# Weights of the next projection loaded from mid-block, and two token tiles multiplied per weight page, in a diffusion block on one core

## The chip, the core and the metric

The kernel runs on one core of one Trainium2 chip. TensorE (PE in the profile) multiplies into PSUM, of which the kernel keeps eight tiles of 128 x 512 float32 here (called banks below); VectorE (DVE), ScalarE (ACT) and GpSimd (POOL) do the rest; the sync engine (SP) issues nearly all transfers, from one queue. The order of the instructions on each engine is fixed when the program is built, so an instruction that waits holds up what stands behind it on its engine. The metric is the device time of one execution in microseconds (us); lower is better.

## What is computed

One layer of a diffusion backbone over 1024 latent tokens and 256 context tokens, width 1024. What matters here is its first third:

```python
mod = jax.nn.silu(c) @ w_mod[layer] + b_mod[layer]        # 6 rows of 1024; and the same for c_ctx
h = modulate(rmsnorm(x, norm1_g[layer]), sh1, sc1)        # 1024 tokens
hc = modulate(rmsnorm(ctx, norm1_g[layer]), sh1c, sc1c)   # 256 tokens
(q_na, k_na, v_na, q_g, k_g, v_g, og, z_lr, m_a, m_b) = jnp.split(h @ w_in[layer], IN_OFFSETS, axis=-1)
q_na = rmsnorm(heads(q_na, NA_HEADS), na_q_norm_g[layer])   # k_na likewise, also for the context
z = jnp.einsum('bldr,drk->bldk', z_lr, w_alpha) + b_alpha   # GLA gates, two directions
la = jnp.maximum(jax.nn.log_sigmoid(z) / GLA_GATE_TAU, GLA_LOG_ALPHA_MIN)   # then cumulated along each chunk
```

Behind it come neighbourhood attention, gated linear attention, the merge, and a SwiGLU network, none of which the change touches.

## The kernel before

Every float32 product is made of three products of a high and a low part (`mm3`): hi·hi, hi·lo and lo·hi. One 128 x 1024 slice of weights comes as a "page": a transfer into a tile `raw` (three buffers), a cast to `w_hi` on ScalarE and a subtraction to `w_lo` on VectorE, both written into tiles with the tag `w`.

The token-major projections are five jobs, `q`, `k`, `v`, `gqk` and `gv`, each 512 columns of `w_in` in four pages (two of the eight steps `k` of the inner dimension per page). Job `q` goes over 8 token tiles of 128, the others over 10 (the last two are context). For one token tile, TensorE runs 24 matmuls of 512 columns (8 steps times 3) into one PSUM bank, tile `psj`; the result then goes through ScalarE and VectorE, for `q` and `k` a norm per head (`norm_heads`: square `sq`, sum, a power on GpSimd, product `st`, copy), and is stored to DRAM. At the start of a job its four pages are loaded and split. The pool `wp` has eight `w` tiles, of which three pages take six (a high and a low part each), and the fourth page takes the two of the pool `jp`. So the next job's page 0 can be split while a job runs, and its other pages only as the running job's last token tile is done with pages 0, 1 and 3.

Two strands of side work are woven in, one step of each per token tile from job `k` on. `mod_units` sums four rows of the modulation vector, each over eight pages `wm` of `w_mod` on VectorE (`acc`), and after the eighth splits the sum into `parts`, adds over partitions with four matmuls (tile `mp`, one PSUM bank) and copies the row out (`mr`). `gate_units` first loads the low-rank gate input (`za`) and the gate weights (`w2r`) and splits them, then makes for each of four `a` three matmuls (tile `psl`, the same bank as `mp`), a clamp on VectorE (`la`), exponential and logarithm on ScalarE, cumulated sums (`cum`) on VectorE, and exponentials again. A scheduler sets the final order of each engine from the order in which the program is written and from its own estimates.

Of the kernel before, what the change touches and what calls it, by code (L numbers as in the profile page):

```python
# [10 lines left out]
F32 = mybir.dt.float32  # L11
# [7 lines left out]
P = 128  # L19
# [3 lines left out]
KT = D // P  # L23
NT = T // P
# [21 lines left out]
NWX = 1  # L46
# [28 lines left out]
CX = 1  # L75
ZH = 4
MID = 6
FK = 1
FQ = 1
FE_ = 1  # L80
# [12 lines left out]
def hybrid_block_kernel(  # L93
# [115 lines left out]
            src, hi = src[part], hi[part]  # L209
        (lo_eng or DVE).tensor_tensor(lo, src, hi.bitcast(F32), op=ALU.subtract)  # L210

    def load_page(pl, src, k0, per, ncols, tag, scale_row=None, lo_eng=None, after=None, bufs=8):
        raw = rawp.tile([P, per, ncols], F32, tag="raw", name="raw")
        SP.dma_start(raw, src[k0 * P:(k0 + per) * P, :].rearrange("(k p) n -> p k n", p=P))
        if scale_row is not None:
            POOL.tensor_tensor(raw, raw, scale_row.unsqueeze(1).broadcast_to([P, per, ncols]), op=ALU.mult)  # L216
        hi = pl.tile([P, per, ncols], F32R, tag=tag, name="w_hi", bufs=bufs)
        lo = pl.tile([P, per, ncols], F32R, tag=tag, name="w_lo", bufs=bufs)
        hi_lo(hi, lo, raw, lo_eng, after)
        return hi, lo  # L220
# [6 lines left out]
    def cut(w, s):  # L227
        return (lambda k: w[0](k)[:, s]), (lambda k: w[1](k)[:, s])

    def mm3(ps, ks, st, mv, first=True, last=True):  # L230
        sh, sl = st
        vh, vl = mv
        ks = list(ks)
        for k in ks:
            PE.matmul(ps, sh(k), vh(k), start=first and k == ks[0], stop=False)
            PE.matmul(ps, sh(k), vl(k), start=False, stop=False)
            PE.matmul(ps, sl(k), vh(k), start=False, stop=last and k == ks[-1])
# [14 lines left out]
    with ExitStack() as sa:  # L252
# [11 lines left out]
        jps = sa.enter_context(pool("jps", NJ, space=PSUM))  # L264

        def h_tok(t):
            if t < NT:
                s = slice(t * P, (t + 1) * P)
                return (lambda k: hh[:, k, s]), (lambda k: hl[:, k, s])
            s = slice((t - NT) * P, (t - NT + 1) * P)  # L270
            return (lambda k: hch[:, k, s]), (lambda k: hcl[:, k, s])
# [102 lines left out]
        mps = sa.enter_context(pool("mps", space=PSUM))  # L374
        jpb = sa.enter_context(pool("jpb", 7 - NJ, space=PSUM))
# [27 lines left out]
        def mod_units():  # L403
            for s in range(4):
                acc = jp.tile([P, D], F32, tag="acc", name="acc", bufs=1)
                POOL.memset(acc, 0.0)
                SP.dma_start(acc[0:1], b_row[0:1, (2 + s) * D:(3 + s) * D])
                for k in range(KT):
                    wm = jp.tile([P, D], F32, tag="wm", name="wm2", bufs=3)
                    SP.dma_start(wm, w_mod[k * P:(k + 1) * P, (2 + s) * D:(3 + s) * D])  # L410
                    DVE.scalar_tensor_tensor(acc, wm, cs[:, k, 0:1], acc, op0=ALU.mult, op1=ALU.add)
                    if k == KT - 1:
                        for c in range(2):
                            c_ = slice(c * 512, (c + 1) * 512)
                            parts = [page("parts", F32R, tag=tg) for tg in ("st", "sb")]
                            hi_lo(parts[0], parts[1], acc[:, c_])
                            mp = mps.tile([P, 512], F32, tag="mp", name="mp2")
                            for u in range(2):
                                PE.matmul(mp, ones_r, parts[u], start=u == 0, stop=u == 1)
                            mr = page("mr2", tag="sb")  # L420
                            ACT.copy(mr[0:1], mp[0:1])
                            SP.dma_start(mod_d[s:s + 1, c_], mr[0:1])
                    yield


        def gate_stream():
            wz_raw = jp.tile([P, KT, 32], F32, name="wz_raw", bufs=1)
            SP.dma_start(wz_raw, w_in[:, 3072:3104].rearrange("(k p) n -> p k n", p=P))
            wz = jp.tile([P, KT, 64], F32R, name="wz", bufs=1)
            hi_lo(wz[:, :, 0:32], wz[:, :, 32:64], wz_raw)  # L430
            for a, b, n, i0, o in ((hh, hl, 512, 0, 0), (hh, hl, 512, 512, 512), (hch, hcl, 256, 0, 1024)):
                ps = jps.tile([P, 512], F32, tag="j", name="psz")
                for k in range(KT):
                    PE.matmul(ps[0:64, 0:n], wz[:, k, :], a[:, k, i0:i0 + n], start=k == 0, stop=False)
                    PE.matmul(ps[0:64, 0:n], wz[:, k, :], b[:, k, i0:i0 + n], start=False, stop=k == KT - 1)
                sz = jp.tile([P, 512], F32, tag="sq", name="sz")
                ACT.copy(sz[0:64, 0:n], ps[0:64, 0:n])
                DVE.tensor_tensor(sz[0:32, 0:n], sz[0:32, 0:n], sz[32:64, 0:n], op=ALU.add)
                SP.dma_start(z_d[:, o:o + n], sz[0:32, 0:n])
# [29 lines left out]

        def gate_units():  # L470
            gate_parts()
            yield
            for a in range(4):
                back = a % 2
                w2a = w2[:, 2 * a:2 * a + 2].rearrange("p h k -> p (h k)")
                la = jp.tile([P, T + TC], F32, tag="la", name="la", bufs=1)
                for o, n in ((0, 512), (512, 512), (1024, 256)):
                    ps = mps.tile([P, 512], F32, tag="mp", name="psl")
                    PE.matmul(ps[:, 0:n], w2a, zs[:, o:o + n], start=True, stop=True)
                    DVE.tensor_scalar(la[:, o:o + n], ps[:, 0:n], ba[:, a:a + 1], -40.0, op0=ALU.add, op1=ALU.max)  # L480
                    yield
                ACT.activation(la, la, AF.Exp, scale=-1.0)
                ACT.activation(la, la, AF.Ln, bias=1.0)
                yield
                DVE.tensor_scalar(la, la, 1.0 / 16.0, 1.0, op0=ALU.mult, op1=ALU.min)
                cum = jp.tile([P, T + TC], F32, tag="cum", name="cum", bufs=1)
                st_ = slice(None, None, -1) if back else slice(None)
                for o, n, r in ((0, 512, rst), (512, 512, rst), (T, TC, ones[:, 0:1].broadcast_to([P, TC]))):
                    DVE.tensor_tensor_scan(cum[:, o:o + n][:, st_], r, la[:, o:o + n][:, st_], 0.0,
                                           op0=ALU.mult, op1=ALU.add)  # L490
                yield
                nl = small.tile([P, 1], F32, tag="nl", name="nl")
                end = T if back else T + TC - 1
                DVE.tensor_scalar_mul(nl, cum[:, end:end + 1], -1.0)
                ein = jp.tile([P, T + TC], F32, tag="la", name="ein", bufs=1)
                ACT.activation(ein[:, 0:T], cum[:, 0:T], AF.Exp)
                ACT.activation(ein[:, T:], cum[:, T:], AF.Exp, bias=nl)
                SP.dma_start(ein_d[a * P:(a + 1) * P, :], ein)
                ex = cum[:, 0:T]
                ACT.activation(ex, ex, AF.Exp, scale=-1.0)  # L500
                SP.dma_start(ex_d[a * P:(a + 1) * P, :], ex)
                yield

        gus = gate_units()
        mus = mod_units()
        nj = 0
        for job, c0 in (("q", 0), ("k", 512), ("v", 1024), ("gqk", 1536), ("gv", 2048)):
            if job == "q":
                w = qw
            else:  # L510
                pages = [load_page(jp if i >= 4 - NWX else wp, w_in[:, c0:c0 + 512], 2 * i, 2, 512, "w",
                                   bufs=2 * NWX if i >= 4 - NWX else 8)
                         for i in range(4)]
                w = [(lambda k, u=u, pages=pages: pages[k // 2][u][:, k % 2, :]) for u in range(2)]
            if job == "k":
                gate_stream()
            for t in range(NT if job == "q" else NT + NTC):
                if job != "q":
                    next(mus, None)
                    next(gus, None)  # L520
                half = job == "gqk" and t >= NT
                n0 = 256 if half else 0
                if job == "q" and t < NPRE:
                    ps = pre[t]
                else:
                    nj += 1
                    ps = (jps, jpb)[nj % 2].tile([P, 512], F32, tag="j", name="psj")
                    mm3(ps[:, n0:], range(KT), h_tok(t), cut(w, slice(n0, 512)))
                if job == "q":
                    norm_heads(ps, q_d, t)  # L530
                elif job == "k":
# [983 lines left out]
```

## Time and profile before

| | |
|---|---|
| runs shown (3) | median 1658.98 us, 1656.54 to 1659.48 |
| the profiled execution | 1664.38 us, of which the span is 1662.6 |
| mean granted clock of TensorE over the span | 0.975 |
| busy share of the span: PE, DVE, ACT, POOL | 94%, 61%, 38%, 32% |
| the chain that ended last: PE, DVE, DMA, ACT, issue, POOL | 68%, 12%, 8%, 4%, 4%, 3% |
| bytes moved, mean rate | 231.30 MB, 139 GB/s |

The profiled execution is 5.40 us over the median of the runs shown. A granted clock of 1.00 is TensorE's upper level, 2.4 GHz, and 0.50 the lower, 1.2 GHz. The matmul ends in the trace are modelled, so a busy TensorE need not be one at its full rate: start times are what to count from.

### The profile page before, as it was taken

The numbers are of one execution on the slowest core, as the hardware profiler recorded it, in microseconds if no ns is written. First come the engines' busy times: TensorE is split into PE (matmuls) and PEld (weight loads), VectorE is DVE, ScalarE is ACT, GpSimd is POOL, SyncE is SP. The second block draws the span as 40 slices with busy tenths as digits, with TensorE's granted clock in tenths as the row PEclk, the third lists the DMA queues.
The fourth block names the chain that finished last, engine by engine and source line by source line (L and its number), as shares of the span: only waits on it lengthen the run. The fifth ranks groups of instructions, "written<-read, shape, count | busy, mean of one in ns | idle before, by whom it ended". The sixth has DMA issues, their size and how long they took to land.

```text
span 1662.6 us, 21554 instructions
## 1 busy us (share of the span) xinstructions
PE 1566.1 (94%) x7884; PEld 1267.2 (76%) x7884; DVE 1017.9 (61%) x1584; ACT 635.4 (38%) x1219; POOL 532.2 (32%) x354
## 2 busy tenths in 40 slices
PE   6999598999999999999989997999999999999998
PEld 4777376887878787778877875788888888887886
DVE  5755546407877774564457568766666666678356
ACT  4333342217877773222211323333333333344442
POOL 2422000003111211210022335455555555256444
PEclk9999699999999999999999997999999999999999
DMA  9445675425333316335553221232323333684342
GB/s 322 134 146 180 218 226 184 145 81 158 108 108 105 115 52 212 116 136 172 204 184 113 77 88 47 89 107 96 102 95 104 111 113 122 219 287 146 102 146 95
DMA packets 166291, 231.30 MB, mean 139 GB/s; under 512 B 15324, under 2 KB 101276, under 8 KB 166184
## 3 DMA queue, kind: packets, MB, share of 16 engines
q1 hardware_dynamic: 166184, 229.91, 42.9%
q8 instruction: 62, 1.02, 0.3%
q14 instruction: 45, 0.37, 0.1%
HBM read 164.68 MB, written 65.19 MB: 138 GB/s over the span
## 4 chain that ended last, share of the span: by engine, by line
PE 68%; DVE 12%; DMA 8%; ACT 4%; issue 4%; POOL 3%; SPq 1%; DVEq 0%; ACTq 0%; POOLq 0%
PE psdn L136 9%; PE psj L136 9%; PE psd L136 9%; PE fZ L136 7%; PE fX L136 7%; PE fW L136 7%; PE pso L136 5%; PE psb L136 3%; PE fY L136 3%; PE pv L136 2%; DMA raw<-in_w_in_dram 2%; PE pt L136 1%; DMA wm<-in_w_mod_dram 1%; PE mp L136 1%; DVE w_lo L210 1%
## 5 line engine op out<-in xcount | busy, mean ns | idle before, releaser
L136 PE MATMUL psdn<-wd,a 128*128 128x512 f32 x924 | 211.8, 390 | 3.4 <-DVE a L210 1.5
L136 PEld LDWEIGHTS psdn<-wd,a 128*128 128x128 f32 x924 | 172.8, 188 | 42.2 <-DVE a L210 3.4
L210 POOL TENSOR_TENSOR w_P<-sc,w_P 128x512 fp32r<-128x512 f32 x88 | 126.5, 1439 | 107.8 <-ACT w_P L205 100.7
L136 PE MATMUL psj<-w_hi,hh 128*128 128x512 f32 x320 | 129.9, 409 | 12.8 <-ACT w_hi L205 12.4
L210 POOL TENSOR_TENSOR w_lo<-raw,w_hi 128x1024 fp32r<-128x1024 f32 x24 | 57.5, 2398 | 249.2 <-ACT w_hi L205 192.8
L136 PE MATMUL fZ<-T,w_P 128*128 128x512 f32 x528 | 130.6, 397 | 5.6 <-DVE u L1267 5.6
L136 PE MATMUL psd<-hh,w_hi 128*128 128x512 f32 x320 | 134.7, 421 | 0.0
L136 PE MATMUL fX<-B,w_P 128*128 128x512 f32 x528 | 131.7, 398 | 0.7 <-ACT u L1086 0.7
L136 PE MATMUL psj<-w_lo,hh 128*128 128x512 f32 x320 | 129.7, 406 | 2.0 <-DVE w_lo L210 2.0
L210 POOL TENSOR_TENSOR w_P<-raw,w_P 128x512 fp32r<-128x512 f32 x66 | 101.9, 1546 | 90.5 <-ACT w_P L205 90.5
L136 PE MATMUL psd<-hh,w_lo 128*128 128x512 f32 x320 | 128.9, 403 | 0.0
L136 PE MATMUL psd<-hl,w_hi 128*128 128x512 f32 x320 | 128.4, 401 | 0.0
L136 PE MATMUL psj<-w_hi,hl 128*128 128x512 f32 x320 | 127.8, 404 | 0.0
L136 PEld LDWEIGHTS fZ<-T,w_P 128*128 128x128 f32 x528 | 101.1, 192 | 28.6 <-DVE u L1267 6.9
L136 PEld LDWEIGHTS fX<-B,w_P 128*128 128x128 f32 x528 | 100.0, 190 | 24.4 <-ACT u L1086 1.1
L205 ACT CAST w_P<-sc 128x512 fp32r<-128x512 f32 x88 | 54.3, 620 | 138.8 <-PE fZ L136 79.7
L205 ACT CAST w_hi<-raw 128x1024 fp32r<-128x1024 f32 x64 | 66.6, 1048 | 91.0 <-POOL raw L216 40.6
L243 POOL TENSOR_TENSOR r<-r,nhalf 128x8 f32<-128x8 f32 (+1 forms) x40 | 50.5, 1266 | 147.9 <-DVE r L242 147.9
L210 DVE TENSOR_TENSOR a<-ar,a 128x512 fp32r<-128x512 f32 x77 | 60.8, 798 | 59.9 <-ACT a L205 59.6
L205 ACT CAST a<-ar 128x512 fp32r<-128x512 f32 x77 | 47.8, 621 | 112.9 <-PE psdn L136 63.6
L136 PEld LDWEIGHTS psj<-w_hi,hh 128*128 128x128 f32 x320 | 62.2, 195 | 29.3 <-ACT w_hi L205 13.8
L210 DVE TENSOR_TENSOR w_lo<-raw,w_hi 128x1024 fp32r<-128x1024 f32 x40 | 53.0, 1331 | 44.0 <-ACT w_hi L205 43.7
(266 smaller groups left out, 3456.1 us busy)
## 6 DMA issues: line engine op xcount, KB each, us to landing
wm<-in_w_mod_dram SPq DMA_DIRECT2D x48, 512.0 KB
raw<-in_w_in_dram SPq DMA_DIRECT2D x40, 512.0 KB
ar<-s_d SPq DMA_DIRECT2D x77, 256.0 KB
raw<-in_w_gate_dram SPq DMA_DIRECT2D x22, 512.0 KB
raw<-in_w_up_dram SPq DMA_DIRECT2D x22, 512.0 KB
s_d<-t1f SPq DMA_DIRECT2D x44, 256.0 KB
s_d<-sa SPq DMA_DIRECT2D x33, 256.0 KB
xt<-in_x_dram SPq DMA_DIRECT2D x16, 512.0 KB
```

What stands on the lines that cost most here:

```text
L136: r = op(*args, **kw)
L205: c = ACT.copy(hi, src)
L210: (lo_eng or DVE).tensor_tensor(lo, src, hi.bitcast(F32), op=ALU.subtract)
L243: POOL.tensor_tensor(r, r, nhalf[:, 0:w], op=ALU.pow)
```

## The change

Four things. In the middle of a job (token tile 5, `AHEAD`) three of the four transfers of the next job's pages are issued (`load_raw`, `NAHEAD`); their casts stay at the start of the next job in the program, and the scheduler places them. Two token tiles are multiplied together: for each page, the six matmuls of the one tile and then the six of the other, into two PSUM banks (`multiply_tokens`), instead of all 24 of one tile and then all of the next. The end of a modulation row (split, four matmuls, copy) is set one token tile later. The gate strand skips job `k`, waits two more token tiles (`GW8`), issues the three `psl` matmuls of one `a` in one step, and takes their banks from the pool of `psj`. No arithmetic is added or removed.

```diff
--- before.py
+++ after.py
@@ -75,6 +75,9 @@
 CX = 1
 ZH = 4
 MID = 6
+GW8 = 2
+AHEAD = 5
+NAHEAD = 3
 FK = 1
 FQ = 1
 FE_ = 1
@@ -209,9 +212,14 @@
             src, hi = src[part], hi[part]
         (lo_eng or DVE).tensor_tensor(lo, src, hi.bitcast(F32), op=ALU.subtract)
 
-    def load_page(pl, src, k0, per, ncols, tag, scale_row=None, lo_eng=None, after=None, bufs=8):
+    def load_raw(src, k0, per, ncols):
         raw = rawp.tile([P, per, ncols], F32, tag="raw", name="raw")
         SP.dma_start(raw, src[k0 * P:(k0 + per) * P, :].rearrange("(k p) n -> p k n", p=P))
+        return raw
+
+    def load_page(pl, src, k0, per, ncols, tag, scale_row=None, lo_eng=None, after=None, bufs=8, raw=None):
+        if raw is None:
+            raw = load_raw(src, k0, per, ncols)
         if scale_row is not None:
             POOL.tensor_tensor(raw, raw, scale_row.unsqueeze(1).broadcast_to([P, per, ncols]), op=ALU.mult)
         hi = pl.tile([P, per, ncols], F32R, tag=tag, name="w_hi", bufs=bufs)
@@ -410,6 +418,7 @@
                     SP.dma_start(wm, w_mod[k * P:(k + 1) * P, (2 + s) * D:(3 + s) * D])
                     DVE.scalar_tensor_tensor(acc, wm, cs[:, k, 0:1], acc, op0=ALU.mult, op1=ALU.add)
                     if k == KT - 1:
+                        yield
                         for c in range(2):
                             c_ = slice(c * 512, (c + 1) * 512)
                             parts = [page("parts", F32R, tag=tg) for tg in ("st", "sb")]
@@ -469,16 +478,17 @@
 
         def gate_units():
             gate_parts()
-            yield
+            for _ in range(GW8):
+                yield
             for a in range(4):
                 back = a % 2
                 w2a = w2[:, 2 * a:2 * a + 2].rearrange("p h k -> p (h k)")
                 la = jp.tile([P, T + TC], F32, tag="la", name="la", bufs=1)
                 for o, n in ((0, 512), (512, 512), (1024, 256)):
-                    ps = mps.tile([P, 512], F32, tag="mp", name="psl")
+                    ps = jps.tile([P, 512], F32, tag="j", name="psl")
                     PE.matmul(ps[:, 0:n], w2a, zs[:, o:o + n], start=True, stop=True)
                     DVE.tensor_scalar(la[:, o:o + n], ps[:, 0:n], ba[:, a:a + 1], -40.0, op0=ALU.add, op1=ALU.max)
-                    yield
+                yield
                 ACT.activation(la, la, AF.Exp, scale=-1.0)
                 ACT.activation(la, la, AF.Ln, bias=1.0)
                 yield
@@ -504,28 +514,47 @@
         gus = gate_units()
         mus = mod_units()
         nj = 0
-        for job, c0 in (("q", 0), ("k", 512), ("v", 1024), ("gqk", 1536), ("gv", 2048)):
+        jobs = (("q", 0), ("k", 512), ("v", 1024), ("gqk", 1536), ("gv", 2048))
+        ahead = []
+        for ji, (job, c0) in enumerate(jobs):
             if job == "q":
                 w = qw
             else:
                 pages = [load_page(jp if i >= 4 - NWX else wp, w_in[:, c0:c0 + 512], 2 * i, 2, 512, "w",
-                                   bufs=2 * NWX if i >= 4 - NWX else 8)
+                                   bufs=2 * NWX if i >= 4 - NWX else 8, raw=ahead.pop(0) if ahead else None)
                          for i in range(4)]
                 w = [(lambda k, u=u, pages=pages: pages[k // 2][u][:, k % 2, :]) for u in range(2)]
             if job == "k":
                 gate_stream()
+            banks = {}
+
+            def multiply_tokens(ts):
+
+                nonlocal nj
+                for t in ts:
+                    nj += 1
+                    banks[t] = (jps, jpb)[nj % 2].tile([P, 512], F32, tag="j", name="psj")
+                for k2 in range(0, KT, 2):
+                    for t in ts:
+                        n0 = 256 if job == "gqk" and t >= NT else 0
+                        for k in (k2, k2 + 1):
+                            mm3(banks[t][:, n0:], [k], h_tok(t), cut(w, slice(n0, 512)), first=k == 0, last=k == KT - 1)
+
             for t in range(NT if job == "q" else NT + NTC):
                 if job != "q":
                     next(mus, None)
-                    next(gus, None)
+                    if job != "k":
+                        next(gus, None)
+                if t == AHEAD and ji + 1 < len(jobs):
+                    c1 = jobs[ji + 1][1]
+                    ahead = [load_raw(w_in[:, c1:c1 + 512], 2 * i, 2, 512) for i in range(NAHEAD)]
                 half = job == "gqk" and t >= NT
-                n0 = 256 if half else 0
                 if job == "q" and t < NPRE:
                     ps = pre[t]
                 else:
-                    nj += 1
-                    ps = (jps, jpb)[nj % 2].tile([P, 512], F32, tag="j", name="psj")
-                    mm3(ps[:, n0:], range(KT), h_tok(t), cut(w, slice(n0, 512)))
+                    if t not in banks:
+                        multiply_tokens([t, t + 1])
+                    ps = banks[t]
                 if job == "q":
                     norm_heads(ps, q_d, t)
                 elif job == "k":
```

The order of three engines near the border of jobs `k` and `v` shows what moves. First SP's queue, in job `k`, up to the loads of job `v`'s weights (`raw`); `k_d` and `kc_d` are the stores of job `k`'s latent and context tiles, `ein_d` and `ex_d` results of the gate strand. Before:

```order
L385 DMA k_d<-st 8x8x1024 x2
L410 DMA wm_1369<-in_w_mod_dram 128x1024
L385 DMA k_d<-st 8x8x1024 x2
L410 DMA wm_1436<-in_w_mod_dram 128x1024
L389 DMA kc_d<-st 128x1024
L422 DMA mod_d<-mr_1379 1x512
L422 DMA mod_d<-mr_1389 1x512
L407 DMA acc<-in_b_row_dram 1x1024
L410 DMA wm_1478<-in_w_mod_dram 128x1024
L389 DMA kc_d<-st 128x1024
L214 DMA raw<-in_w_in_dram 128x2x512 x3
L410 DMA wm_1544<-in_w_mod_dram 128x1024
L410 DMA wm_1578<-in_w_mod_dram 128x1024
L214 DMA raw<-in_w_in_dram 128x2x512
```

After the change:

```order
L393 DMA k_d<-st 8x8x1024 x4
L418 DMA wm_1261<-in_w_mod_dram 128x1024
L217 DMA raw<-in_w_in_dram 128x2x512 x2
L393 DMA k_d<-st 8x8x1024 x4
L217 DMA raw<-in_w_in_dram 128x2x512
L418 DMA wm_1282<-in_w_mod_dram 128x1024
L393 DMA k_d<-st 8x8x1024 x4
L418 DMA wm_1347<-in_w_mod_dram 128x1024
L418 DMA wm_1446<-in_w_mod_dram 128x1024
L217 DMA raw<-in_w_in_dram 128x2x512
```

All four `raw` now stand among the stores of the earlier token tiles, and the gate strand's two stores are gone from the job.

Next ScalarE, from the split of the first modulation row (`parts`) to the first cast of a `v` page (`w_hi`) before, and to the last one after. Before:

```order
L205 CAST parts<-acc 128x512 x2
L421 COPY mr_1379<-mp_1376 1x512
L421 COPY mr_1389<-mp_1386 1x512
L400 COPY st<-st 128x8x64
L482 ACTIVATE la<-la 128x1280
L483 ACT_TABLE_LOAD
L483 ACTIVATE la<-la 128x1280
L496 ACT_TABLE_LOAD
L496 ACTIVATE ein<-cum 128x1024
L205 CAST w_hi<-raw 128x1024
```

After the change (`w_hi` for page 0 stands further ahead, and is not in these rows):

```order
L408 COPY st<-st 128x8x64
L208 CAST parts<-acc 128x512 x2
L208 CAST w_hi<-raw 128x1024
L430 COPY mr_1369<-mp_1366 1x512
L408 COPY st<-st 128x8x64
L430 COPY mr_1379<-mp_1376 1x512
L208 CAST w_hi<-raw 128x1024
L401 ACTIVATE sq<-psj 128x512
L208 CAST w_hi<-raw 128x1024
```

The casts no longer stand behind the gate strand's exponentials (`la`, `ein`); page 1's stands behind `parts`.

Last TensorE, where the first row's sum is added over partitions (`mp`). Before, the last three matmuls of job `k`, the side work and the first of job `v`:

```order
L136 MATMUL psj<-w_lo,hch 128x512
L136 MATMUL psj<-w_hi,hcl 128x512
L136 MATMUL mp_1376<-parts,ones_r 128x512 x2
L136 MATMUL mp_1386<-parts,ones_r 128x512 x2
L136 MATMUL psl<-zs,w_736 128x512 x2
L136 MATMUL psl<-zs,w_736 128x256
L136 MATMUL psl<-zs,w_736 128x512
L136 MATMUL psj<-w_hi,hh 128x512 x2
```

After, inside the last pair of token tiles of job `k`:

```order
L139 MATMUL psj<-w_hi,hch 128x512
L139 MATMUL mp_1366<-parts,ones_r 128x512
L139 MATMUL psj<-w_lo,hch 128x512
L139 MATMUL psj<-w_hi,hcl 128x512
L139 MATMUL mp_1366<-parts,ones_r 128x512
L139 MATMUL psj<-w_hi,hch 128x512
L139 MATMUL psj<-w_lo,hch 128x512
```

The four `mp` moved from the border into the last pair, behind its 13th matmul; the gate strand's `psl` moved away, to the 76th matmul of job `v`, as three in a row.

## Rows read from the trace of the kernel before

**Rows 1.** Stretches of the projections: us, busy us and instructions of each engine, granted clock, DMA.

```profile
core 0: us, PE busy (x) PEld busy (x) DVE busy (x) ACT busy (x) POOL busy (x), PEclk, DMA share, GB/s
101.20:164.80 63.60, 58.45 (x245) 46.26 (x243) 30.15 (x48) 21.34 (x32) 14.80 (x9) 0.97 0.52 162
164.80:190.40 25.60, 5.76 (x10) 2.23 (x9) 12.85 (x18) 11.07 (x14) 2.95 (x3) 0.57 0.62 224
190.40:252.00 61.60, 61.24 (x253) 48.81 (x254) 30.11 (x30) 22.25 (x28) 0.95 (x1) 0.96 0.71 227
252.00:310.60 58.60, 53.70 (x240) 43.14 (x239) 38.49 (x56) 15.42 (x19) 0.95 (x1) 0.94 0.49 165
310.60:367.20 56.60, 56.60 (x249) 46.05 (x248) 3.46 (x4) 9.85 (x16) 4.81 (x2) 1.00 0.25 82
```

**Rows 2.** Waits of TensorE, 95 to 380 us: total us, times, longest us.

```profile
PE psj L136 <- ACT w_hi L205: 12.4, 2, 10.0
PE mp L136 <- ACT parts L205: 6.2, 1, 6.2
PE mp L136 <- ACT mr L421: 3.9, 2, 3.2
PE psl L136 <- DVE w L210: 2.5, 1, 2.5
PE psl L136 <- DVE la L480: 2.3, 3, 0.8
PE psj L136 <- DVE w_lo L210: 2.0, 4, 0.8
```

**Rows 3.** Timeline of TensorE: start us, us, what [idle before <-releaser].

```profile
130.50 0.50 PE L136 MATMUL psl<-zs,w 96*128 96x512 f32 x1 [2.49 <-DVE w L210]
...
171.02 1.54 PE L136 MATMUL mp<-parts,ones_r 128*128 128x512 f32 x2 [6.20 <-ACT parts L205]
...
175.16 0.80 PE L136 MATMUL psl<-zs,w 96*128 96x512 f32 x1 [0.66 <-ACT mr L421]
...
190.39 1.22 PE L136 MATMUL psj<-w_hi,hh 128*128 128x512 f32 x2 [9.99 <-ACT w_hi L205]
...
275.25 0.79 PE L136 MATMUL mp<-parts,ones_r 128*128 128x512 f32 x1 [3.17 <-ACT mr L421]
```

**Rows 4.** Stretches just behind three of these waits, columns as in rows 1.

```profile
130.50:134.50 4.00, 4.00 (x11) 3.12 (x12) 2.12 (x5) 0.00 (x0) 1.64 (x1) 0.57 0.51 162
171.00:180.40 9.40, 5.73 (x8) 2.23 (x8) 4.85 (x8) 2.97 (x5) 2.84 (x2) 0.50 0.49 152
275.20:281.00 5.80, 5.75 (x14) 4.49 (x15) 0.00 (x0) 0.57 (x1) 0.20 (x1) 0.50 0.53 208
```

**Rows 5.** Timeline of ScalarE around the end of job k.

```profile
152.39 0.59 ACT L393 ACTIVATE sq<-psj 128x512 f32<-128x512 f32 x1
...
170.35 1.14 ACT L205 CAST parts<-acc 128x512 fp32r<-128x512 f32 x2 [0.58 <-DVE acc L411]
...
188.35 1.06 ACT L496 ACTIVATE ein<-cum 128x1024 f32<-128x1024 f32 x1 [3.62 <-DVE cum L489]
189.31 1.03 ACT L205 CAST w_hi<-raw 128x1024 fp32r<-128x1024 f32 x1
```

**Rows 6.** Timeline of VectorE around the end of job k.

```profile
155.72 0.69 DVE L398 TENSOR_TENSOR st<-psj,r 128x512 f32<-128x512 f32 x1 [1.82 <-POOL r L243]
...
169.03 1.28 DVE L411 SCALAR_TENSOR_TENSOR acc<-wm,cs,acc 128x1024 f32<-128x1024 f32 x1 [0.45 <-DMA wm<-in_w_mod_dram]
```

**Rows 7.** Timeline of SP's queue of transfers: issue time, us of issuing.

```profile
114.76 3.67 SPq L458 DMA_DIRECT2D za<-z_d  x8
123.68 3.90 SPq L465 DMA_DIRECT2D w2r<-in_w_alpha_dram  x6
...
160.04 2.79 SPq L410 DMA_DIRECT2D wm<-in_w_mod_dram  x1
...
176.62 2.36 SPq L214 DMA_DIRECT2D raw<-in_w_in_dram  x3
```

**Rows 8.** Instructions of the down product (tile psdn) in one stretch, columns as in rows 1.

```profile
core 0: us, PE busy (x) PEld busy (x) DVE busy (x) ACT busy (x), PEclk, DMA share, GB/s
1480.00:1540.00 60.00, 59.49 (x260) 48.13 (x259) 5.02 (x8) 0.00 (x0) 1.00 0.57 186
```

## The prediction

> **What bounds the kernel now.** I first cut the stage of the projections, from job `k`'s first matmul (101.2 us) to the first matmul behind job `gv` (367.2), at the borders of its jobs [rows 1]. The reader is to see that TensorE is busy nearly all the time in every stretch but one: between 164.8 and 190.4 it works 5.8 us of 25.6. Job `gv`, with no side work left but four `mp` matmuls, is the measure: 240 + 4 matmuls of 512 columns in 56.6 us, 0.232 us each, at a granted clock of 1.00. At that price the other stretches hold this much work and so much that is lost:
>
> Job `k` (240 `psj` and three `psl`, one of them half as wide): 242.5 x 0.232 = 56.3 of 63.6, lost 7.3. The border (four `mp`, four `psl`): 7.5 x 0.232 = 1.7 of 25.6, lost 23.9. Job `v` (240, four `mp`, four `psl`): 57.4 of 61.6, lost 4.2. Job `gqk` (192 and 48 of half width, four `mp`, a half `psl`): 220.5 x 0.232 = 51.2 of 58.6, lost 7.4. Together 42.8 us, and the work 223.2 of the 266.0.
>
> Then I asked for TensorE's waits in that stage [rows 2]: 12.4 us for the cast of weights (`w_hi`) in two waits, 6.2 for `parts`, 3.9 for the copies that free the one `mp` bank, 2.5 and 2.3 in the gate strand, 2.0 for `w_lo`: 29.3. The timeline puts them at the start of `k` (12.4 less the 10.0 of the next: 2.4), at the first `psl` (2.5), at the border (6.2 and 10.0, with small ones between), and in `gqk` (3.2) [rows 3]. The other 13.5 us lie behind the waits: granted 0.57 or 0.50 there, 14 matmuls take 5.8 us behind the wait in `gqk`, 0.41 each [rows 2 to 4].
>
> Last, what the border waited for [rows 5 to 7]. The last page of the first modulation row is issued at 160.04 and VectorE can add it only at 169.03, 9.0 us later; `parts` follow at 170.35. The next job's `raw` is issued at 176.62, behind the copies of the row; its cast starts at 189.31, because ScalarE has it behind the exponentials of the gate strand (`ein` 188.35).
>
> **What the change does, part by part.** It adds no arithmetic, so the 223.2 us of work stay and only the 42.8 can move.
>
> *Start of `k`.* The fourth page's transfer now stands one group of stores earlier on SP, and with pairs page 3 is wanted after 36 matmuls, not 18: 8.4 us after the start instead of 4.2. The wait of 2.4 goes. So does the gate strand from `k`, with its 2.5 and the slow 4.0 us behind it.
>
> *The first modulation row, now in the last pair of `k`.* With `k` undisturbed from 101.2, the pair of tiles 4 and 5 ends at 101.2 + 144 x 0.232 = 134.6. One norm takes 4.0 us from `sq` to the end of `st` (152.39 to 156.41) [rows 5, 6]; the two of a pair go one after the other, so the second store is out some 9 us later, at 143.5, and behind it SP issues the eighth `wm`. It lands between 4.7 us later (an estimate: its 512 KB and the 512 KB of the store ahead of it, at the 224 GB/s of the border [rows 1]) and 9.0 later (as at 160.04): 148.2 to 152.5. The add (1.28) and the first of two casts (0.6 of 1.14) make it 150.1 to 154.4; TensorE comes to `mp` at 101.2 + (192 + 13) x 0.232 = 148.8. So a wait of 1.3 to 5.6; behind it the bank's copy and the second low part cost about one more. I take 3.5 with the slow clock, since the transfers of the gate strand, which stood ahead of the 9 us one, are gone from `k`; bounds 0 and 9.8 (6.2, 0.7 and 0.7 at the border and the slow matmuls with them). Queued behind `mp` is the rest of the last pair. `k` then loses 3.5 instead of 7.3.
>
> *The border.* Page 0 of `v` is cast in mid `k`; page 1 stands behind `parts`, is ready between 153 and 157 and wanted at about 164, 2.8 us into `v`; page 2 needs only page 1 of `k` let go, 24 matmuls into the last pair; page 3 must wait for the end of `k`, but is wanted 8.4 us later, and a cast (1.03) and a subtraction are 2.5. The loads are 20 us ahead. So the 23.9 go, down to nothing. If ScalarE were late by more than those 7 us, each us more would be one of TensorE.
>
> *The gate strand in `v`.* Its loads of `za` stand behind the store of `k`'s last tile. That tile's norm is held up by page 3's cast and subtraction and two adds of `wm` (1.28 each) in VectorE's order; I count 10.5 us after the end of `k`. Four `za` issues (3.67 for eight) 1.9, six `w2r` 3.9, and from there to `psl` what it took before (127.58 to 130.50) 2.9: 19.2 [rows 3, 7]. TensorE comes to `psl` after 75 matmuls, 17.4. A wait of 1.8, and the slow stretch as before [rows 4]: 4.2 in all. Bounds 0 and 10 (two late `wm` in front of the norm). Behind it is the rest of tiles 2 and 3.
>
> *The second row, in the last pair of `v`.* Here `parts` stand on ScalarE behind the exponentials of the strand's second `a`, whose `psl` come just before the pair of tiles 6 and 7. Before, it took 13.2 us from the first `psl` (175.16) to `ein` (188.35), 10.9 without TensorE's 2.3 of waits [rows 2, 3, 5]. Three exponentials of up to 1.06, a copy and a cast more make 14.3; TensorE is there after 50 matmuls and three `psl`, 12.3. A wait of 2.0, taken as 2.3 and bounded by 0 and 6.2. The 4.2 lost now are mostly slow matmuls behind the wait at the border, and go with it; so `v` loses 4.2 at the gate strand and 2.3 here, 6.5 against 4.2.
>
> *`gqk`.* The waits for `w_lo` at its start (most of the 2.0) go, as pages 1 and 2 are let go in the last pair. The third row's second half waits, as now, for the copy that frees the `mp` bank, behind the exponentials of the fourth `a`: the same sum, against 54 matmuls: about 2, with the clock 2.9; bounds 0 and 6.2. So 2.9 instead of 7.4. `gv` has no wait now and gets none.
>
> *Two banks in turn.* The rows say that changing banks is free: the down product changes banks every third matmul, and runs 260 of them in 60 us, 0.231 each, at 1.00 [rows 8]. The Trainium skill (TensorE: Matmul & The Clock Gate, section A second HAM failure mode: psum-queue depth-cycling) tells of a kernel in which cycling through PSUM banks made the engine idle briefly between groups, so often that its clock went up and down. By that rule the pairs would pay; by the row they don't, and the sum goes by the row.
>
> **The sum.** k -3.8, border -23.9, v +2.3, gqk -4.5: -29.9 us. Against the profiled execution, 1664.4 - 29.9 = 1634.5; against the median of the runs shown, which is 5.4 lower, **1629**.
>
> **The rivals.** *All hidden:* the four remaining waits are nothing; 42.8 us gone, 1616. For it speaks that each is only 2 to 4 us; against it that each chain comes out later than TensorE by its own rows. *Old waits at new places:* the modulation and gate chains are as late as at their bounds (9.8, 10, 6.2, 6.2, together 32.2): 42.8 - 32.2 = 10.6, 1648; about half way, 1640. For it speaks the 9.0 us landing of a `wm`; against it that SP's queue is shorter in `k`. *The change does nothing:* the time is given back behind 367.2, where attention starts on loads queued behind `gv`'s last store: 1659. Against it: these loads follow that store before and after, and the DMA engines are only a quarter busy in `gv`. *Slower:* the change of banks drops the clock. A matmul at the lower level cost 0.41 instead of 0.232 (above), so 0.18 more; the paired matmuls are 96 in `q`, three times 240, 192, and 48 halves counted as 24: 1032, at most 186 us, which makes 1629 + 186 = 1815. It decides from 29.9 / 0.18 = 166 such matmuls on, a sixth of them; there it is slower than now. Against it the down product's rows.
>
> **How the numbers follow.** My sum, 1622 to 1636: 0.60. All hidden, 1614 to 1621: 0.12. Old waits at new places, 1637 to 1648: 0.20. Nothing, 1656 to 1662: 0.04. Slower: 0.04. A measurement of this kernel can tell about 0.2%, 3.3 us, from no change. So faster 0.92, same 0.04, slower 0.04. The range runs from all hidden to two thirds into the third case, 1615 to 1645.
>
> **What would show it.** Right: no wait for `w_hi` at the starts of `k` and `v`; job `v` starting near 161 instead of 190; first matmul behind `gv` near 337; waits left at `mp` in the last pairs of `k` and `v` and in `gqk`, and at the first `psl`, of 2 to 4 us each; nothing changed in length behind the projections. Wrong: a wait of 6 us or more at one `mp` or `psl`, a granted clock below 0.95 in `v` or `gqk` without a wait ahead of it, or attention starting late.

## The result, and the profile after

Measured: 1627.62 us, median of four runs (1627.48 to 1632.9), against 1658.24 for the kernel before in the runs beside them. By the medians that is 30.6 us less, where 29.9 was forecast; the ratio on record is 0.9824, with a 95% interval of 0.9802 to 0.9846.

The stage of the projections first, cut at the borders of its jobs as in [rows 1] (us, busy us and instructions of each engine, granted clock, DMA share, GB/s):

```profile
core 0: us, PE busy (x) PEld busy (x) DVE busy (x) ACT busy (x) POOL busy (x), PEclk, DMA share, GB/s
101.80:164.30 62.50, 57.93 (x247) 47.02 (x246) 26.95 (x40) 17.62 (x30) 15.25 (x9) 0.97 0.61 198
164.30:227.40 63.10, 59.39 (x252) 47.55 (x251) 34.95 (x43) 30.23 (x38) 4.23 (x3) 0.97 0.59 196
227.40:283.20 55.80, 53.76 (x252) 44.67 (x251) 41.48 (x62) 21.41 (x24) 0.95 (x1) 0.97 0.65 221
283.20:339.10 55.90, 55.90 (x245) 45.63 (x244) 10.45 (x10) 11.88 (x18) 4.80 (x2) 1.00 0.39 128
```

It is four stretches now, not five. The border of 25.6 us between `k` and `v` is no stretch of its own any more: job `v` starts at 164.2 (the cut stands at 164.3), not 190.4. The stage takes 237.3 us where it took 266.0, with as many matmuls, so 28.7 us less. At the price of 0.232 us for a matmul of 512 columns, with which the prediction counted, the stretches now lose 5.9 us in `k` (244 matmuls, 56.6 of 62.5), 5.3 in `v` (249, 57.8 of 63.1) and 3.6 in `gqk` (225, 52.2 of 55.8), and `gv` takes 0.7 less than the price; the sum is 14.1 where 42.8 were lost before and 12.9 forecast.

TensorE's waits in the stage answer to [rows 2]; here is all of it (total us, times, longest us):

```profile
PE mp L139 <- ACT parts L208: 5.8, 2, 4.6
PE psl L139 <- DVE w L213: 2.5, 1, 2.5
PE mp L139 <- ACT mr L430: 2.0, 1, 2.0
```

10.3 us in four waits, against 29.3. No wait for `w_hi` or `w_lo` is left. Where they stand, as in [rows 3] (start us, us, what, idle time before and what ended it):

```profile
153.46 0.80 PE L139 MATMUL mp<-parts,ones_r 128*128 128x512 f32 x1 [4.57 <-ACT parts L208]
...
184.00 1.30 PE L139 MATMUL psl<-zs,w 96*128 96x512 f32 x3 [2.45 <-DVE w L213]
...
215.59 0.50 PE L139 MATMUL mp<-parts,ones_r 128*128 128x512 f32 x1 [1.25 <-ACT parts L208]
...
265.12 0.50 PE L139 MATMUL mp<-parts,ones_r 128*128 128x512 f32 x1 [2.04 <-ACT mr L430]
```

These are the four places named ahead: the first modulation row in the last pair of `k`, the gate strand's first `psl` in `v`, the second row in the last pair of `v`, and the second half of the third row in `gqk`. Behind three of them the clock is low as it was in [rows 4]:

```profile
153.50:157.00 3.50, 3.50 (x9) 2.79 (x10) 1.97 (x5) 2.50 (x4) 1.94 (x1) 0.52 0.21 85
184.00:187.60 3.60, 3.60 (x9) 2.88 (x10) 2.13 (x4) 1.66 (x2) 0.00 (x0) 0.53 0.84 251
265.10:269.50 4.40, 4.38 (x12) 3.48 (x13) 1.58 (x4) 0.57 (x1) 0.95 (x1) 0.61 0.85 331
```

Nine matmuls in 3.5 us behind the first, 0.39 each, at a granted clock of 0.52. Behind the third wait, 1.25 us long, no slow matmuls follow.

What the first wait waited for, on SP, VectorE and ScalarE, beside [rows 5 to 7]:

```profile
139.44 5.02 SPq L393 DMA_DIRECT2D k_d<-st  x4
144.50 2.18 SPq L418 DMA_DIRECT2D wm<-in_w_mod_dram  x2
```

```profile
151.47 1.28 DVE L419 SCALAR_TENSOR_TENSOR acc<-wm,cs,acc 128x1024 f32<-128x1024 f32 x1 [2.69 <-DMA wm<-in_w_mod_dram]
...
156.28 0.68 DVE L213 TENSOR_TENSOR parts<-acc,parts 128x512 fp32r<-128x512 f32 x1
```

```profile
152.78 1.14 ACT L208 CAST parts<-acc 128x512 fp32r<-128x512 f32 x2 [3.31 <-DVE acc L419]
153.83 1.04 ACT L208 CAST w_hi<-raw 128x1024 fp32r<-128x1024 f32 x1
...
158.56 1.05 ACT L208 CAST w_hi<-raw 128x1024 fp32r<-128x1024 f32 x1
```

The last page of the row is issued at 144.50 with its neighbour, behind the stores of tiles 4 and 5, and added at 151.47: 7.0 us, against 9.0 before. `parts` follow at 152.78, and the casts of `v`'s pages 1 and 2 at 153.83 and 158.56, both well ahead of 164.3.

### The profile page after: what moved, and what is told of

Its sections match the earlier page's. It is cut to its first block, busy times and chain, and to the rows that moved or that the text cites. A ratio compares the mean times of both kernels' runs of the same rounds, so it can differ in the third digit from the quotient of the medians.

```text
span 1625.7 us, 21566 instructions
## 1 busy us (share of the span) xinstructions
PE 1549.0 (95%) x7884; PEld 1258.1 (77%) x7884; DVE 1020.0 (63%) x1584; ACT 635.8 (39%) x1219; POOL 532.6 (33%) x354
## 4 chain that ended last, share of the span: by engine, by line
PE 70%; DVE 12%; DMA 6%; issue 4%; ACT 4%; POOL 3%; SPq 1%; DVEq 0%; ACTq 0%; POOLq 0%
PE psdn L139 9%; PE psj L139 9%; PE psd L139 9%; PE fZ L139 7%; PE fX L139 7%; PE fW L139 7%; PE pso L139 5%; PE psb L139 3%; PE fY L139 3%; PE pv L139 2%; PE pt L139 1%; DMA q_d<-st 1%; DMA wm<-in_w_mod_dram 1%; DMA raw<-in_w_in_dram 1%; POOL r L251 1%
## 5 line engine op out<-in xcount | busy, mean ns | idle before, releaser
L139 PEld LDWEIGHTS fZ<-T,w_P 128*128 128x128 f32 x528 | 101.1, 192 | 28.7 <-DVE u L1296 6.9
L213 DVE TENSOR_TENSOR a<-ar,a 128x512 fp32r<-128x512 f32 x77 | 65.7, 864 | 58.8 <-ACT a L208 58.8
L208 ACT CAST w_P<-raw 128x512 fp32r<-128x512 f32 x66 | 40.9, 621 | 91.0 <-PE fW L139 63.9
```

Source lines behind the costliest of these rows:

```text
L139: r = op(*args, **kw)
L208: c = ACT.copy(hi, src)
```

## The experiments

Each of the first four kernels is the kernel before with one of the four parts of the change alone; the next three undo one part of the changed kernel; then come kernels that go further. Beside the ratio to the kernel before (95% interval), the start of the first matmul behind `gv` in the profiled execution is given, since it cuts off what happens later: 367.2 before, 339.1 in the changed kernel.

**Early loads alone.** Edit to the kernel before:

```diff
...
+                if t == AHEAD and ji + 1 < len(jobs):
+                    c1 = jobs[ji + 1][1]
+                    ahead = [load_raw(w_in[:, c1:c1 + 512], 2 * i, 2, 512) for i in range(NAHEAD)]
...
```

> The kernel before with the early loads alone. Theory (the border between k and v held TensorE because the next weights were issued and cast behind the modulation row and the gate strand's exponentials; whatever puts them ahead of these removes it): the order has three loads in k and the casts of pages 0 to 2 ahead of the row's split, so the border's 23.9 us and the wait at the start of k go, the gate strand's 4 us in k stays: 1632 to 1640 us. Rival one (pairs are needed, since only they let the old pages go early enough): a wait of 8 us or more for w_hi stays at the start of v, 1645 or more. Rival two (the gate strand's move is what counts): 1650 or more.

Measured: 1628.94 us, ratio 0.9806 (0.9788 to 0.9823), first matmul behind `gv` at 338.4. All of the gain, from one part, and 3 us below the range of the theory. TensorE's waits in the stage:

```profile
PE psj L139 <- DVE w_lo L213: 3.1, 3, 1.8
PE psj L139 <- ACT w_hi L208: 2.5, 2, 2.3
PE psl L139 <- DVE la L488: 2.2, 2, 1.3
PE psl L139 <- DVE w L213: 0.8, 1, 0.8
```

The 2.3 at the start of `k` stayed, which the theory had go; the border's waits are gone, and there is no wait for `mp` at all. SP's queue, and ScalarE around the border, show why:

```profile
147.02 2.07 SPq L217 DMA_DIRECT2D raw<-in_w_in_dram  x3
```

```profile
157.40 1.04 ACT L208 CAST w_hi<-raw 128x1024 fp32r<-128x1024 f32 x1
...
160.71 1.05 ACT L208 CAST w_hi<-raw 128x1024 fp32r<-128x1024 f32 x1 [0.51 <-PE psj L139]
...
163.57 1.04 ACT L208 CAST w_hi<-raw 128x1024 fp32r<-128x1024 f32 x1
...
171.28 1.14 ACT L208 CAST parts<-acc 128x512 fp32r<-128x512 f32 x2 [1.11 <-DVE acc L419]
...
182.95 1.05 ACT L208 CAST w_hi<-raw 128x1024 fp32r<-128x1024 f32 x1
...
186.86 1.06 ACT L504 ACTIVATE ein<-cum 128x1024 f32<-128x1024 f32 x1 [1.56 <-DVE cum L497]
```

With the three loads issued at 147.02, ahead of job `k`'s last stores and not behind them at 176.62 [rows 7], the scheduler put the casts of three pages (157.40, 160.71, 163.57) ahead of the row's split `parts` and of the strand's exponentials, and the fourth (182.95) in the midst of these. The four `mp` moved too: they now follow 32 matmuls into `v`, and `parts` at 171.28 are in time for them. The rival that pairs are needed falls, and so does the one of the gate strand.

**Pairs alone.** The kernel before with `multiply_tokens([t, t + 1])` and nothing else.

> The kernel before with two token tiles per weight page alone. Theory: the loads of v stay behind the stores of k, four mp and four psl stay at the border, so it stays: 1648 to 1657 us, with only the waits for w_lo and the start of k gone. Rival one (pairs are needed and do most): 1640 or less. A cost of changing banks would show as 1665 or more, with a granted clock under 0.95 in the jobs.

Measured: 1654.12 us, 0.9952 (0.9933 to 0.9971), first matmul behind `gv` at 360.3. TensorE's waits:

```profile
PE mp L139 <- ACT parts L208: 6.1, 1, 6.1
PE psl L139 <- DVE la L488: 5.0, 4, 2.7
PE psl L139 <- DVE w L213: 4.4, 1, 4.4
PE psj L139 <- DVE w_lo L213: 4.0, 1, 4.0
PE psj L139 <- ACT w_hi L208: 4.0, 1, 4.0
```

The border is still there (6.1 for `parts`, then the strand's clamps, then 4.0 and 4.0 for the weights). It is not the casts' place behind `ein` that keeps it here:

```profile
176.24 1.88 SPq L217 DMA_DIRECT2D raw<-in_w_in_dram  x3
```

```profile
183.42 1.98 ACT L208 CAST w_hi<-raw 128x1024 fp32r<-128x1024 f32 x2
...
190.76 1.06 ACT L504 ACTIVATE ein<-cum 128x1024 f32<-128x1024 f32 x1 [4.07 <-DVE cum L497]
```

Two casts stand ahead of the strand's `ein`, but the loads are still issued at 176.24, and job `v` starts at 184.5. The change of banks at every sixth matmul costs nothing to be seen.

**The row later alone.** The kernel before with the one `yield` ahead of `for c in range(2)`.

> The kernel before with the end of a modulation row one token tile later alone. Theory: four mp stay at the border, behind them the loads: 1654 to 1661 us, no change to be told. A rival (the row's last page, 9 us in landing, is what starts the border, so a token tile of 5.5 us more hides it): 1645 to 1652.

Measured: 1650.38 us, 0.9938 (0.9917 to 0.9958), first matmul behind `gv` at 356.7. The theory had said no change; the time is in the rival's range, but not for the rival's reason, since the wait for `parts` is still 6.0 us. ScalarE at the border:

```profile
182.14 1.03 ACT L205 CAST w_hi<-raw 128x1024 fp32r<-128x1024 f32 x1
183.19 1.28 ACT L497 ACT_TABLE_LOAD   x1
187.16 1.06 ACT L497 ACTIVATE ein<-cum 128x1024 f32<-128x1024 f32 x1 [2.69 <-DVE cum L490]
```

Here the first cast of a page (182.14) stands between the strand's logarithm and its exponentials (187.16), where it stood behind the first of these before (189.31, behind `ein`) [rows 5]. The longest wait for `w_hi` is 4.0 us instead of 10.0, job `v` starts at 183.2 instead of 190.4, and a wait of 4.1 for a `w_lo` comes up behind it. The three loads are issued at 176.62, as before; what the earlier place of the cast, with one `psl` less at the border, was worth to the start of `v` is these 7.2 us. Moving the row by one token tile changed the scheduler's place for a cast on another engine.

**The gate strand later alone.** The kernel before with the strand's four edits:

```diff
+GW8 = 2
...
-            yield
+            for _ in range(GW8):
+                yield
...
-                    ps = mps.tile([P, 512], F32, tag="mp", name="psl")
+                    ps = jps.tile([P, 512], F32, tag="j", name="psl")
...
-                    yield
+                yield
...
-                    next(gus, None)
+                    if job != "k":
+                        next(gus, None)
```

> The kernel before with the gate strand's move alone (no step in k, two token tiles later, three psl in one step, other banks). Theory: no exponentials in k, the casts stand behind the row but ahead of the strand: 1634 to 1643 us, the mp waits and a start of v of some us left. Rival one (pairs needed): 1645 or more.

Measured: 1629.37 us, 0.9807 (0.979 to 0.9824), first matmul behind `gv` at 340.4. Again nearly all of the gain, from another part alone; nearly 5 us under the lowest that was expected. SP's queue, where these loads were issued at 176.62 before:

```profile
155.52 1.06 SPq L215 DMA_DIRECT2D raw<-in_w_in_dram  x1
...
162.21 3.04 SPq L215 DMA_DIRECT2D raw<-in_w_in_dram  x2
```

They are out ahead of the end of job `k` here too, the row's four `mp` stand inside `k` (from 144.91), and no exponentials of the strand come before 191. Job `v` starts at 167.1; what is left is mostly 6.7 us of waits for `w_hi`, in four, and 2.4 for the `mp` bank.

**The early loads undone** in the changed kernel (`if False and t == AHEAD ...`).

> The changed kernel with the early loads undone. The early loads alone and the gate strand's move alone each gave all of the gain; so theory: each is enough, and without the early loads the order still has the four loads among the stores of k, since no exponentials stand there: 1625 to 1634 us, within 0.4% of the changed kernel. Rival: the two add up: 1636 or more.

Measured: 1628.59 us, 0.9819 (0.9797 to 0.9841), first matmul behind `gv` at 342.7. No difference to be told from the changed kernel.

**The gate strand's move undone** in the changed kernel (the four edits above taken back).

> The changed kernel with the gate strand as before. Theory (each is enough): no wait at the border, the strand's first wait of some 2.5 us back in k and gone from v, the first row's matmuls now 31 into v and so without their wait: 1620 to 1632 us. Rival (the two add up): 1636 or more.

Measured: 1628.53 us, 0.9813 (0.9793 to 0.9834), first matmul behind `gv` at 334.6. No difference either by the whole time; its stage is 232.9 us long in the profiled execution, against 237.3 in the changed kernel's. Its first `psl` waits 4.5 us in `k`, where some 2.5 was expected, and the row 1.9 in `v`, where no wait was.

**Pairs undone** in the changed kernel (`multiply_tokens([t])`).

> The changed kernel with one token tile at a time. Theory: pairs give little once the border is gone; pages 1 to 3 are let go later, so small waits for w_hi and w_lo of 1 to 3 us come at the starts of the jobs: 1626 to 1636 us. Rival (pairs hide the casts at the borders): a wait of 5 us or more at the start of v or gqk, 1638 or more.

Measured: 1635.82 us, 0.9864 (0.9845 to 0.9882), first matmul behind `gv` at 345.2. The pairs are worth about 0.4% here, at the very end of what was expected, and not where the rival had them: no wait at the start of `v` or `gqk`. TensorE's two longest entries, and VectorE where the first row ends:

```profile
PE mp L139 <- ACT parts L208: 9.1, 2, 6.8
PE psj L139 <- ACT w_hi L208: 2.6, 1, 2.6
```

```profile
156.97 2.60 DVE L419 SCALAR_TENSOR_TENSOR acc<-wm,cs,acc 128x1024 f32<-128x1024 f32 x2 [4.67 <-DMA wm<-in_w_mod_dram]
```

The row's last two pages are added one behind the other from 156.97 (two adds in one entry), after a wait of 4.67 for a transfer; the last add starts at 158.3, 6.8 us later than in the changed kernel, and `mp` waits 6.8 us instead of 4.6; the start of `k` has its 2.6 back.

**Rows and gate strand later still.** The changed kernel with a second `yield` ahead of a row's end, and `GW8 = 4`.

> The changed kernel with the end of a modulation row one more token tile later and the gate strand two more tiles later. The waits left (mp in the last pairs of k and v and in gqk, 4.6, 1.3 and 2.0 us, and 2.5 at the first psl) with the slow matmuls behind them hold some 16 us. Theory (each is a chain that is late by its own few us, so a later place hides it): 1612 to 1622 us. Rival (the chain moves with its place, and a wait comes up elsewhere): 1625 to 1632.

Measured: 1623.74 us, 0.9789 (0.9759 to 0.9819), first matmul behind `gv` at 331.3: between the ranges of theory and rival. The stage is 8 us shorter than in the changed kernel, with no wait at `psl` and 6.0 us in all at `mp`, with the row's end moved by one token tile and the strand by two.

Then four kernels beside each other on one chip, in five rounds. **The changed kernel again:**

> The changed kernel again, beside the three that follow on the same chip: 1624 to 1632 us. Theory of the spread (the clock sometimes falls behind a wait of 2 us and sometimes not): the waits are the same to 0.3 us, the slow matmuls behind them and behind the later stages' waits need not be.

Measured: 1628.95 us (1626.31 to 1629.25), 0.9812 (0.9786 to 0.9837). The four waits are 3.75, 2.54, 1.38 and 2.05 us: three the same to 0.15, the first 0.8 shorter, so more apart than expected.

**The later version again:**

> Rows and gate strand later still, again, with more rounds: 1619 to 1626 us, faster than the changed kernel by 4 us or more if the waits left at the first psl and at the first mp were its cost; rival (they move elsewhere): within 3 us of it.

Measured: 1625.45 us (1617.98 to 1628.47), 0.979 (0.976 to 0.9821); first matmul behind `gv` at 333.0 against 338.0. By the median 3.5 us faster than the changed kernel, between the 4 of the theory and the 3 of the rival, but the runs overlap: not settled by the whole time, though the stage itself is shorter in both profiled executions.

**The same with free banks for `mp`:**

```diff
-        mps = sa.enter_context(pool("mps", space=PSUM))
-        jpb = sa.enter_context(pool("jpb", 7 - NJ, space=PSUM))
+        jpb = sa.enter_context(pool("jpb", 8 - NJ, space=PSUM))
...
-                            mp = mps.tile([P, 512], F32, tag="mp", name="mp2")
+                            mp = jps.tile([P, 512], F32, tag="j", name="mp2")
```

> The same, with the mp tiles taken from the banks of psj, so that a row's second half waits for no copy. Theory (the copy that frees the one mp bank is the last wait in v and gqk): the waits on mr, 3.2 us in all, go; 1617 to 1623 us. Rival (the bank was only the first of two things in time, the low part of the row or the copy's place on ScalarE the other): the wait turns into one for parts, same as e10.

Measured: 1619.26 us (1617.32 to 1625.88), 0.9765 (0.9739 to 0.9792); first matmul behind `gv` at 328.7. The waits for the copy are gone; the one wait left grew from 2.8 to 4.4 us and is for the row's second low part. So theory and rival each hold for a part. VectorE shows what that part stands behind:

```profile
152.96 0.68 DVE L213 TENSOR_TENSOR parts<-acc,parts 128x512 fp32r<-128x512 f32 x1
...
155.78 1.22 DVE L213 TENSOR_TENSOR w_lo<-raw,w_hi 128x1024 fp32r<-128x1024 f32 x1
157.55 1.23 DVE L213 TENSOR_TENSOR w_lo<-raw,w_hi 128x1024 fp32r<-128x1024 f32 x1 [0.55 <-ACT w_hi L208]
...
161.39 0.69 DVE L405 TENSOR_TENSOR st<-psj,r 128x512 f32<-128x512 f32 x1 [1.81 <-POOL r L251]
162.00 0.68 DVE L213 TENSOR_TENSOR parts<-acc,parts 128x512 fp32r<-128x512 f32 x1
```

First low part at 152.96, second at 162.00: between them a norm's end, two `w_lo` of the next job's pages, and the next norm, 1.8 us of it waiting for GpSimd. All six runs of this kernel are below all five of the changed one: it is faster than both kernels of this study.

**The row's end three token tiles later** (a third `yield`, and the steps of `mod_units` that are then left run behind the last job)**:**

> The same, with the end of a row three token tiles later instead of two. Theory (the low part of the first row on VectorE, 2.8 us, is late because two weight pages stand ahead of it, and has 2 to 6 us more here): no wait of TensorE over 1 us before the attention stage, its first matmul near 326, 1613 to 1620 us. Rival: the row's end meets the next chain and a wait of 2 us or more comes up.

Measured: 1622.36 us (1614.72 to 1628.17), 0.9773 (0.9743 to 0.9804); first matmul behind `gv` at 329.8. The wait for the second low part is 4.5 us, not under 1: the theory falls, and the rival's wait came. With the place in the program moved the scheduler put that part behind three `w_lo` (155.62, 157.39 and 161.84) instead of two, and it starts at 163.57. The runs overlap those of the kernel above, so no difference in time is told.

## Why the prediction was right

*The border* (-23.9): right, and shown. No `w_hi` is waited for at the start of `v`. But of what took it away the prediction told only that all parts together do. The runs show that the early loads alone or the gate strand's move alone give nearly all of it, and that either can be taken back from the changed kernel at no cost that can be told: 0.9806 and 0.9807 alone, 0.9819 and 0.9813 undone. What both have in common is two things at once: the transfers of three `v` pages are issued before `k` ends (at 147.02; at 155.52 and 162.21), and their casts stand ahead of ScalarE's exponentials. The first counts for more. Before, the transfers were issued at 176.62, 11.8 us after the end of `k` at 164.8, so no place of the casts could take away that part of the 25.6 us. With the loads as late and a cast ahead of `ein` (the row later alone, the pairs alone) `v` still starts at 183.2 and 184.5, and most of the border stays. No run has early loads with the casts left behind the exponentials, so what the second is worth by then is not shown.

*Job `k`* (-3.8, loss of 3.5 left): a loss of 5.9 was left. The mechanism was right to the row, the last page's landing 7.0 us lay inside 4.7 to 9.0 and the wait of 4.57 inside 1.3 to 5.6; the term was sized at the low end, and the slow matmuls behind it are the rest. The 2.4 at its start went, as said, and the runs say by which part: with the pairs alone it is gone, and with them undone it is back. Of the two things named ahead the earlier place of the load is enough: the fourth page is issued at 88.54 in the changed kernel, and its `w_lo`, 1.23 us from 98.18, is done before `k` starts at 101.8; with the pairs undone it is issued at 100.71 and cast at 107.56. So the later need of page 3 wasn't called on.

*The gate strand in `v`* (4.2): a wait of 2.45, forecast 1.8, and slow matmuls behind it; the excess over full speed is 4.2.

*The second row* (2.3) came out at a wait of 1.25 with no slow matmuls; *`gqk`* (2.9 left) lost 3.6, with a wait of 2.04. The 14.3 us on which both these waits were worked out can't be rebuilt exactly from the rows shown, which have only one of the exponentials.

*The sum:* that it came within 1.2 us in the stage (14.1 lost, 12.9 forecast) is in part luck. `k` lost 2.4 more than forecast, `v` 1.2 less (5.3 for 6.5), `gqk` 0.7 more and `gv` 0.7 less. And of the 30.6 us of the medians the stage shows 28.7.

*Two banks in turn:* the rival that the clock would suffer is ruled out for this kernel. Pairs alone are faster than before (0.9952), and `gv` runs its 244 matmuls in 55.9 us at a granted clock of 1.00, where it took 56.6. So the rule of the Trainium skill (TensorE: Matmul & The Clock Gate, section A second HAM failure mode: psum-queue depth-cycling) doesn't show here, with a change of bank at every sixth matmul and no idle time between.

*Behind the projections* nothing was to change. In the two profiled executions it does: 1662.6 - 367.2 = 1295.4 us before, 1625.7 - 339.1 = 1286.6 after. Nothing shows this to be an effect of the change: TensorE is idle as long in both (52.2 and 51.6 us) and takes 1243.2 and 1235.0 us for the same instructions, at a mean granted clock of 0.98 and 0.99. The last section returns to it. The medians do not contain most of it: they differ by 30.6 us, and 28.1 of these are there by the first matmul behind `gv`.

## What to carry to other kernels

Where a job's first matmul waits for a cast, look both at when its load was issued and at what stands ahead of the cast on its engine. Here the load stood behind the copies of side work on one queue and the cast behind its exponentials on another; two quite different edits that changed both orders gave the same 30 us each, and an earlier cast with a late load kept most of the loss. When several edits come together, take each alone before giving it a share; of these, two were each enough and a third was worth 0.4%. A side chain that ends in matmuls on a busy TensorE cost its wait and, behind three of the four waits here, slow matmuls, and moving its place in the program moves it on each engine separately, so look for the instruction it stands behind there.

## What the runs showed of the hardware that was not expected

The clock behind a short wait fell in one execution and not in another. In the attention stage both kernels have the same wait; in the kernel before, with the stretch from 567 to 572 us below it (columns as in [rows 1]):

```profile
567.24 0.74 PE L136 MATMUL pv<-phl,vhl 128*128 128x256 f32 x4 [1.98 <-DVE phl L210]
```

```profile
567.00:572.00 5.00, 4.76 (x19) 4.14 (x20) 2.92 (x11) 3.09 (x11) 0.88 (x1) 0.66 0.29 105
```

And in the changed kernel, with the stretch from 537 to 542:

```profile
537.10 0.74 PE L139 MATMUL pv<-phl,vhl 128*128 128x256 f32 x4 [1.96 <-DVE phl L213]
```

```profile
537.00:542.00 5.00, 4.90 (x30) 4.36 (x31) 2.91 (x12) 4.01 (x13) 0.74 (x1) 1.00 0.38 136
```

A wait of 1.98 us and a granted clock of 0.66 behind it, 19 matmuls in 5 us; a wait of 1.96 us and 1.00, 30 matmuls. Ten of the profiled executions (all but the last kernels, with rows and gate strand later still) have one order of instructions on TensorE behind `gv`; the time from there to the end lies between 1284.6 us (early loads undone: 1627.3 - 342.7) and 1295.4 (before). So some 11 us of one execution may be what the clock did behind waits that are always there, and two executions set side by side cannot show a gain smaller than that in the whole time. A stage's own length shows less spread, though not none: the changed kernel's is 237.3 us in one execution and 235.2 in the other. Medians of several runs help too. The clock goes along with the time: the two longest of the ten, 1295.4 and 1293.4 (the gate strand's move undone), have a mean granted clock of 0.98 there and the shortest 0.99; and of the eleven runs of the kernel before beside the last four kernels, the longest, 1667.14 us, has 0.974 over the whole span and the shortest, 1653.26, has 0.983. That the clock is what makes the whole spread was not tried by itself.
